# Transposes put at once instead of between matmuls, in the opening stage of a two-layer hybrid attention trunk

## The chip, the cores and the metric

One core of one Trainium2 chip runs the whole program. The metric is the device time of one execution in microseconds (us). Lower is better.

## The reference, cut to what matters

x and mem are 256 x 1024 in float32. Two layers, each with three branches on the same normalised input; the memory branch has keys and values that don't depend on x.

```python
for l in range(2):
    h = rmsnorm(x, norm_g[l])
    z = h @ w_in[l]                                  # 1024 x 7968, split into the inputs of the branches
    o_a = sparse_attention(...) * silu(...)
    o_b = forgetting_attention(...) * silu(...)
    mem_kv = rmsnorm(mem, mem_norm_g[l]) @ w_mem_kv[l]   # 1024 x 1024: keys, then values
    o_m = memory_attention(...) * silu(...)
    u = sum of g_i * (o_i @ w_branch_i[l])           # g_i = sigmoid of columns of z
    x = x + u @ w_out[l]
```

## The kernel before, in words

Every large product is done in three passes: an activation and a weight are each split into a high part (`aTh`, `whi`, a rounded copy) and a low part (`aTl`, `wlo`, what is left), and high x high, low x high and high x low are added in PSUM. A weight block of 256 rows is loaded by SyncE's queue into `wraw` (4 buffers), ScalarE writes `whi` (L168) and VectorE `wlo` (L169), 3 buffers each, two blocks ahead of use.

`gemm_steps` (L256) does one block: two row tiles t (128 rows of x or mem each) times two groups of 128 input channels times three passes, so 12 matmuls into one PSUM bank per t. `gemm` calls it four times for 1024 input channels. Tag `mm` has 3 banks, `S` 2, `T` 2, `O` 1. At the end of each step `tick` (L224) advances a clock and runs what `later(d, fn)` has put down as due.

Activations must lie transposed. `put_T` (L212) makes 4 transposes of 128 x 128 on TensorE into one bank of `T` (L220), and after the fourth calls the function that empties the bank: ScalarE writes the high part and VectorE the low part (L398 and L399, for two halves of the bank in turn). Each of these small pieces goes through `put` (L205) into the list `small`. `gemm_steps` hands the list out: after each of its matmuls it issues a share of what is in it (`hand_out`, L200), tied behind that matmul with `tc.issue_after`. `flush` (L196) issues the rest.

The tile framework orders each engine's instructions with a timeline simulation when the kernel is built (`schedule_with_timeline_sim=True`, L1248), so the order on an engine is the program's order as far as operands were ready in that simulation. In the trace it differs in places: matmuls of the values run before the last matmuls of the keys.

The opening stage, up to L643, in the program's order:

- 8 matmuls on zeros (L310), the gains `gk` transposed and copied (L333);
- `mem_norm` (L422): mem arrives in 4 column chunks of 256 channels. The first chunk is transposed at once and flushed. The other three (g = 1, 2, 3) hang on the list `within`: one is put down in the middle of each of the first three steps, between the 6 matmuls of t = 0 and the 6 of t = 1, so that its 4 transposes are handed out behind the matmuls of t = 1;
- `mem_stats` (L438): ScalarE squares the rows of mem (L443);
- `mem_kv` (L447): 4 steps for the keys, 4 for the values. From the keys' banks come squares (L366), a reciprocal root on GpSimd, the normalised keys (L457), and two `put_T` (after steps 5 and 6) whose banks are emptied into `mK` (L374, L376);
- `norm_x` (L629), due after step 1: squares of x (L633), x times its reciprocal root (L635), and four `put_T` after steps 4 to 7, whose banks are emptied into `hT`;
- `need(("h", l))`, and then the matmuls on `hT`: `K2` first, 416 columns wide.

So 9 calls of `put_T` lie between the first step and L643 of layer 0: 3 for mem, 4 for h and 2 for the keys, 36 transposes in all. All later use of `put` (attention units, and layer 1) goes on as it is.

Of the kernel before, what the change touches and what calls it, by code (L numbers as in the profile page):

```python
# [59 lines left out]
def hybrid_kernel(ctx: ExitStack, tc, I, cst_d, out_d):  # L60
# [131 lines left out]


    small = []

    def flush():  # L196
        while small:
            small.pop(0)()
# [6 lines left out]
    def put(*fns):  # L205

        def f():
            for fn in fns:
                fn()
        small.append(f)  # L210

    def put_T(blocks, then):  # L212

        q = []

        def one(i, b):
            if i == 0:
                q.append(pT())
            b = b()
            nc.tensor.transpose(q[0][0:b.shape[1], i * 128:(i + 1) * 128], b, ident)  # L220
        for i, b in enumerate(blocks):
            put(lambda i=i, b=b: one(i, b), *([lambda: then(q[0])] if i == len(blocks) - 1 else []))

    def tick():  # L224
        flush()
        clock[0] += 1
        unit_step()
        due = [c for c in conts if c[0] <= clock[0]]
        conts[:] = [c for c in conts if c[0] > clock[0]]
        for _, fn in due:  # L230
            fn()
# [16 lines left out]
    def need(k):  # L248
        for _ in range(60):
            if k in done_:  # L250
                flush()
                return
            tick()
        raise AssertionError(k)
# [220 lines left out]
    class Out:  # L475
# [4 lines left out]
        def add(self, cols, lhsT, rhs):  # L480
            def f():
                first = self.O is None
                if first:
                    self.O = pO()
                nc.tensor.matmul(self.O[0:lhsT.shape[1], cols], lhsT, rhs, start=first, stop=False,  # L485
                                 skip_group_check=True)
            put(f)

        def close(self):
            self.left -= 1  # L490
            if self.left == 0:
                add = small.pop()
                put(add, lambda: self.done(self.O))
# [80 lines left out]
    for l in range(2):  # L574
# [66 lines left out]
        mKT, mV = mem_kv(l, mT, rm)  # L641
        done_.discard("mem")
        need(("h", l))  # L643


        KH = S([128, 2, 2, T], "KH", dt=F32R)
# [605 lines left out]
```

## Time and profile before

| | |
|---|---|
| median of 3 runs | 646.13 us |
| the three runs | 644.62, 646.13, 646.20 us |
| the profiled execution | 645.26 us |
| its span, first to last instruction | 643.5 us |
| TensorE (PE) busy | 627.2 us, 97% |
| VectorE (DVE) busy | 484.5 us, 75% |
| ScalarE (ACT) busy | 391.8 us, 61% |
| GpSimd (POOL) busy | 173.8 us, 27% |
| mean granted clock of TensorE | 0.992 of full speed |

Times in the rows are us from the start of the span, unless ns is written. In a timeline row stand start, duration, engine, line, operation, what is written <- what is read, the count, and in brackets how long the engine had been idle and what ended that. A line of the program can be that of a helper: all transposes of `put_T` have L220 and all matmuls of `gemm_steps` L266. PE is the matmul side of TensorE, PEclk the granted clock as a share of full speed.

### The profile page before, as it was taken

To read this page: it belongs to the slowest core of one execution; us is meant where nothing else is said; L and a number is where in the kernel's file an instruction comes from. 1 tells how busy PE (TensorE), PEld (TensorE's weight loads), DVE (VectorE), ACT (ScalarE), POOL (GpSimd) and SP (SyncE) were. 2 spreads that over 40 slices of the span, in tenths; PEclk is the share of its full clock that TensorE was granted. 3 is DMA by queue.
4 is the path that set the end of the run, shared out by engine and by line. 5 is a ranking of instruction groups with operands and counts; after the bars stand their busy time and mean duration, and the time that the engine had idled before them with its cause. 6 is when DMAs were issued, how large, how long until landed. Compare 5 with 4: busy or idle time off the path is not lost.

```text
span 643.5 us, 10308 instructions
## 1 busy us (share of the span) xinstructions
PE 627.2 (97%) x3567; PEld 538.2 (84%) x3567; DVE 484.5 (75%) x849; ACT 391.8 (61%) x822; POOL 173.8 (27%) x232
## 2 busy tenths in 40 slices
PE   6889999999999999999999999999999999999997
PEld 4669898878898888888887989988889888888885
DVE  3567899867986886955586698996799688777563
ACT  5476578755667576654467566694467576765441
POOL 2531411441620420602112224122053041142030
PEclk7899999999999999999999999999999999999999
DMA  8746756765444644446754674576545355445542
GB/s 303 170 112 193 216 134 154 222 191 169 128 133 100 190 130 141 133 158 197 226 172 112 194 226 137 154 226 200 139 124 164 99 157 158 144 131 165 163 149 80
DMA packets 75412, 104.51 MB, mean 162 GB/s; under 512 B 16832, under 2 KB 31456, under 8 KB 75360
## 3 DMA queue, kind: packets, MB, share of 16 engines
q1 hardware_dynamic: 75296, 103.84, 55.6%
q8 instruction: 28, 0.46, 0.3%
q14 instruction: 24, 0.20, 0.1%
q10 hardware_dynamic: 64, 0.02, 0.0%
HBM read 102.78 MB, written 1.05 MB: 161 GB/s over the span
## 4 chain that ended last, share of the span: by engine, by line
PE 86%; DVE 6%; issue 2%; ACT 2%; DMA 2%; POOL 1%; SPq 0%; DVEq 0%; ACTq 0%
PE mm L266 60%; PE S L266 6%; PE T L220 5%; PE mm L820 5%; PE O L485 4%; DVE wlo L169 2%; PE S L1005 1%; DMA wraw<-in_w_mem_kv_dram 1%; PE S L1104 1%; PE S L1164 1%; DVE big L790 1%; PE S L911 1%; DVE sg L804 1%; ACT whi L168 1%; PE S L913 1%
## 5 line engine op out<-in xcount | busy, mean ns | idle before, releaser
L169 DVE TENSOR_TENSOR wlo<-wraw,whi 128x1024 fp32r<-128x1024 f32 (+3 forms) x185 | 231.2, 1254 | 88.6 <-ACT whi L168 87.3
L168 ACT ACTIVATE whi<-wraw 128x1024 fp32r<-128x1024 f32 (+3 forms) x185 | 192.3, 1041 | 111.6 <-PE mm L266 64.8
L266 PE MATMUL mm<-whi,aTh 128*128 128x512 f32 (+1 forms) x480 | 189.4, 401 | 7.3 <-ACT aTh L398 4.6
L266 PE MATMUL mm<-whi,aTl 128*128 128x512 f32 (+1 forms) x480 | 190.2, 396 | 1.3 <-DVE aTl L399 1.3
L266 PE MATMUL mm<-wlo,aTh 128*128 128x512 f32 (+1 forms) x480 | 184.4, 397 | 1.0 <-DVE wlo L169 1.0
L540 POOL TENSOR_TENSOR P<-P,d 128x512 f32<-128x512 f32 (+1 forms) x64 | 59.4, 944 | 209.1 <-DVE d L532 115.5
L266 PEld LDWEIGHTS mm<-whi,aTh 128*128 128x128 f32 x480 | 90.5, 190 | 25.4 <-ACT aTh L398 5.9
L266 PEld LDWEIGHTS mm<-wlo,aTh 128*128 128x128 f32 x480 | 91.1, 190 | 18.8 <-DVE wlo L169 1.9
L266 PEld LDWEIGHTS mm<-whi,aTl 128*128 128x128 f32 x480 | 91.1, 190 | 18.1 <-DVE aTl L399 1.7
L820 PE MATMUL mm<-aTh,wlo 128*128 128x256 f32 x192 | 54.8, 287 | 0.0
L820 PE MATMUL mm<-aTh,whi 128*128 128x256 f32 x192 | 54.7, 286 | 0.0
L820 PE MATMUL mm<-aTl,whi 128*128 128x256 f32 x192 | 54.6, 285 | 0.0
L529 ACT ACTIVATE P<-S,m 128x256 f32<-128x256 f32 (+1 forms) x112 | 46.8, 432 | 7.2 <-DVE m L526 6.5
L1078 POOL TENSOR_TENSOR big<-big,t 128x512 f32<-128x512 f32 x16 | 28.2, 1772 | 58.9 <-DVE t L1077 54.0
L374 ACT ACTIVATE PTh<-T 128x512 fp32r<-128x512 f32 (+1 forms) x48 | 26.8, 563 | 24.9 <-PE T L220 24.6
L266 PE MATMUL mm<-whi,oTh 128*128 128x512 f32 x96 | 38.5, 404 | 0.7 <-DVE t L1128 0.4
L266 PE MATMUL mm<-wlo,oTh 128*128 128x512 f32 x96 | 38.8, 407 | 0.0
L266 PE MATMUL mm<-whi,oTl 128*128 128x512 f32 x96 | 38.6, 403 | 0.0
L820 PEld LDWEIGHTS mm<-aTh,wlo 128*128 128x128 f32 x192 | 36.5, 191 | 0.4
L820 PEld LDWEIGHTS mm<-aTh,whi 128*128 128x128 f32 x192 | 36.6, 191 | 0.3
L820 PEld LDWEIGHTS mm<-aTl,whi 128*128 128x128 f32 x192 | 36.6, 191 | 0.2
L526 DVE TENSOR_REDUCE m<-S 128x2 f32<-128x512 f32 (+3 forms) x64 | 32.1, 515 | 2.7 <-PE S L1164 2.5
(236 smaller groups left out, 1030.5 us busy)
## 6 DMA issues: line engine op xcount, KB each, us to landing
wraw<-in_w_in_dram SPq DMA_DIRECT2D x112, 512.0 KB, 3.9
wraw<-in_w_out_dram SPq DMA_DIRECT2D x16, 512.0 KB, 4.1
wraw<-in_w_mem_kv_dram SPq DMA_DIRECT2D x15, 512.0 KB, 4.1
wraw<-in_w_branch_a_dram SPq DMA_DIRECT2D x16, 256.0 KB, 4.0
wraw<-in_w_branch_b_dram SPq DMA_DIRECT2D x8, 512.0 KB, 3.6
wraw<-in_w_branch_m_dram SPq DMA_DIRECT2D x8, 512.0 KB, 3.6
wraw<-in_w_in_dram SPq DMA_DIRECT2D x8, 408.0 KB, 3.2
wraw<-in_w_in_dram SPq DMA_DIRECT2D x8, 384.0 KB, 3.7
```

Source lines behind the costliest of these rows:

```text
L168: nc.scalar.activation(wh[:, j, :n], v[:, j, :n], AF.Copy)
L169: nc.vector.tensor_tensor(wl[:, j, :n], v[:, j, :n], wh[:, j, :n].bitcast(F32), op=ALU.subtract)
L220: nc.tensor.transpose(q[0][0:b.shape[1], i * 128:(i + 1) * 128], b, ident)
L266: mi = nc.tensor.matmul(o_, a[:, kg, ts], w_[:, k, :n], start=(kg == 0 and i == 0), stop=(last and k == 1 and i == 2))
L374: nc.scalar.activation(hi, src, AF.Copy, scale=scale)
L485: nc.tensor.matmul(self.O[0:lhsT.shape[1], cols], lhsT, rhs, start=first, stop=False, skip_group_check=True)
L526: nc.vector.tensor_reduce(m[:, n:n + c], heads(sp[:, o_:o_ + w * c], c), axis=AXX, op=ALU.max, negate=True)
L529: nc.scalar.activation(self.P[:, k], sp[:, k], AF.Exp, bias=m[:, n:n + 1], accum_out=d[:, n:n + 1])
L540: nc.gpsimd.tensor_tensor(P3, P3, b3(d[:, n:n + c], c, w), op=ALU.mult)
L790: nc.vector.tensor_tensor(QA[os_, g, :, ts], q[gs], QA[gs, g, :, ts].bitcast(F32), op=ALU.subtract)
L820: mi = nc.tensor.matmul(o_, w_, a[:, kg, :], start=(kg == 0 and j % 2 == 0 and i == 0), stop=(kg == 7 and i == 2), skip_group_check=True)
L1078: nc.gpsimd.tensor_tensor(uv, uv, tn, op=ALU.add)
```

## The change

A flag `lump` is true at first and becomes false for good after `need(("h", l))` of layer 0. While it is true, `put` issues its piece at once, in program order and tied to no matmul. After that it appends to `small` as before.

```diff
     small = []
+    lump = [True]
...
     def put(*fns):
 
         def f():
             for fn in fns:
                 fn()
-        small.append(f)
+        if lump[0]:
+            f()
+        else:
+            small.append(f)
...
         done_.discard("mem")
         need(("h", l))
+        lump[0] = False
```

## Rows read from the trace of the kernel before

**Rows 1.** The page: busy time of each engine over the span.
```profile
PE 627.2 (97%) x3567; PEld 538.2 (84%) x3567; DVE 484.5 (75%) x849; ACT 391.8 (61%) x822; POOL 173.8 (27%) x232
```
**Rows 2.** Windows: length; busy (count) PE, PEld, DVE, ACT, POOL; PEclk, DMA, GB/s.
```profile
0.00:45.50 45.50, 35.84 (x141) 26.37 (x142) 22.34 (x33) 26.11 (x53) 16.01 (x51) 0.89 0.69 197
...
8.70:15.10 6.40, 6.29 (x16) 4.25 (x16) 3.33 (x4) 4.76 (x9) 0.86 (x3) 0.52 1.04 395
...
22.00:26.70 4.70, 4.70 (x18) 3.46 (x17) 1.71 (x3) 1.43 (x3) 4.03 (x15) 0.67 0.88 126
26.70:33.30 6.60, 6.51 (x33) 5.13 (x31) 2.75 (x5) 3.22 (x9) 0.00 (x0) 1.00 0.79 207
33.30:36.50 3.20, 1.05 (x3) 0.59 (x4) 1.60 (x3) 3.20 (x14) 2.11 (x3) 1.00 0.00 0
```
**Rows 3.** Waits of PE from 3 to 45.5 us: total, times, longest.
```profile
PE mm L266 <- ACT aTh L398: 4.6, 3, 3.0
PE mm L266 <- ACT whi L168: 1.7, 1, 1.7
PE mm L266 <- DVE aTl L399: 1.3, 1, 1.3
PE mm L266 <- DVE wlo L169: 0.5, 1, 0.5
```
**Rows 4.** Timeline of PE in the opening stage.
```profile
8.77 1.22 PE L266 MATMUL mm<-whi,aTh 128*128 128x512 f32 x2 [2.96 <-ACT aTh L398]
...
12.99 0.41 PE L220 MATMUL T<-cst,big 128*128 128x128 f32 x1
...
16.36 0.73 PE L266 MATMUL mm<-whi,aTh 128*128 128x512 f32 x2 [1.31 <-ACT aTh L398]
...
20.86 0.50 PE L266 MATMUL mm<-whi,aTl 128*128 128x512 f32 x1 [1.31 <-DVE aTl L399]
...
32.62 0.60 PE L220 MATMUL T<-cst,t 128*128 128x128 f32 x4
...
45.50 0.43 PE L266 MATMUL mm<-whi,aTh 128*128 128x416 f32 x1
```
**Rows 5.** Timeline of ACT in the same stage.
```profile
12.74 1.04 ACT L443 ACTIVATE t<-big 128x1024 f32<-128x1024 f32 x1
...
15.86 0.45 ACT L398 ACTIVATE aTh<-T,gk 128x256 fp32r<-128x256 f32 x1
...
33.81 1.06 ACT L168 ACTIVATE whi<-wraw 128x1024 fp32r<-128x1024 f32 x1
```
**Rows 6.** Timeline of DVE in the same stage.
```profile
11.91 0.48 DVE L399 SCALAR_TENSOR_TENSOR aTl<-T,gk,aTh 128x256 fp32r<-128x256 f32 x1
...
18.37 0.76 DVE L635 TENSOR_SCALAR t<-x,rx 128x1024 f32<-128x1024 f32 x1 [0.71 <-DMA gcol<-in_fox_q_norm_dram]
19.04 1.38 DVE L169 TENSOR_TENSOR wlo<-wraw,whi 128x1024 fp32r<-128x1024 f32 x1
20.34 0.86 DVE L399 SCALAR_TENSOR_TENSOR aTl<-T,gk,aTh 128x256 fp32r<-128x256 f32 x2
...
36.44 0.68 DVE L457 TENSOR_TENSOR t<-mm,rmk 128x512 f32<-128x512 f32 x1
```
**Rows 7.** The chain that ended last, in order of time, merged pieces (start, length).
```profile
27.77 0.11 PE T L220
...
28.23 4.11 PE mm L266 x18
...
41.42 0.44 PE T L220 x4
```
**Rows 8.** SyncE's queue: the issue of mem's second chunk.
```profile
2.25 0.43 SPq L292 DMA_DIRECT2D big<-in_mem_dram  x1
```
**Rows 9.** DMA issues from 2.2 to 2.4 us: KB, us from issue to landing.
```profile
big<-in_mem_dram SPq DMA_DIRECT2D x1, 256.0 KB, 6.0
```
**Rows 10.** Windows of the matmuls of L266 alone: length; busy (count) PE, PEld; PEclk, DMA, GB/s.
```profile
8.70:32.60 23.90, 20.65 (x60) 12.67 (x60) 0.80 0.84 241
```

## The prediction, made before the change was run

> **What bounds the kernel now.** I read the page first, and from it one thing: TensorE is busy 627.2 of 643.5 us [rows 1], so PE sets the pace and only its own idle or slow time can be won. Next the windows. Of the 16.3 us in which PE isn't busy, 45.50 - 35.84 = 9.7 lie in the first 45.5 us, which is all that the change touches; the remaining 598 us have 6.6 us between them. The windows also show the second loss, the granted clock: 0.52 of full speed from 8.7 to 15.1 us (the lower of the two levels, 1.2 GHz, nearly throughout), and 0.67 from 22.0 to 26.7 [rows 2]. Third the waits of PE in the opening stage: three for the high part of the transposed activations (4.6 us), one for the low part (1.3), one each for a weight's two parts (1.7 and 0.5) [rows 3]. The timelines of PE, ACT and DVE then tell why the operand was late [rows 4 to 6].
>
> The reader should see this chain. Step 1 (keys, block 0) starts at 8.77. The transposes of mem's second chunk are handed out behind the matmuls of its second half and the last starts at 12.99, on a slow clock. By then ACT has gone into the squares of mem at 12.74, and the first half of that chunk is emptied only at 15.86; PE, done with step 1, stands still for 1.31 us until 16.36 [rows 4, 5]. The low part of the next half stands in DVE's queue behind x's normalisation (18.37) and a weight split (19.04) and comes at 20.34; PE stands still another 1.31 us until 20.86 [rows 4, 6]. Then the clock is low again for part of 22.0 to 26.7 [rows 2].
>
> **The change part by part.** It adds and removes no instruction and no DMA. It moves 36 transposes (9 calls of `put_T`) from "behind matmul n of the next half step" to "as early as the operand and the bank of tag `T` allow", ahead of those matmuls in the program's order. SyncE's queue gets nothing before or after anything else from it, and GpSimd neither. What moves with the transposes is the emptying on ACT and DVE.
>
> The transposes themselves: in the chain one between matmuls costs 0.11 us and four in a row cost 0.44, 0.11 each [rows 7]. So lump or not is worth 0; I take 0.
>
> *a, chunk 2 of mem.* Its data lie in memory at 2.25 + 6.0 = 8.25 us [rows 8, 9], inside the wait of 2.96 us that ends at 8.77 [rows 4]. At the low clock I double the 0.11 us: four transposes are 0.9 us that leave step 1. From 8.25 they would end near 9.1 and push the first matmul by up to 0.35. I take 0.5 us won, bounds 0 and 0.9.
>
> *b, the wait of 1.31 us before 16.36.* With the transposes done near 9, ACT can empty the bank before it enters the squares at 12.74, where it now comes behind them. Full removal is 1.3. If the first half still falls behind the squares, it is at best the first thing after two of them, 1 us sooner than 15.86. I take 1.0, bounds 0 and 1.3.
>
> *c, the waits of 0.35 (the third of the three for the high part, 4.6 - 2.96 - 1.31) and 1.31 us up to 20.86.* The second half of chunk 2 no longer waits; but chunk 3 goes into the bank that chunk 1 leaves after 11.91 + 0.48 = 12.4 us [rows 6], its emptying still meets squares on ACT and the split at 19.04 on DVE, and so a wait may come back one step later. I take half of 1.66: 0.8, bounds 0 and 1.66.
>
> *d, the low clock in 22.0 to 26.7.* At a mean of 0.67, (1 - 0.67) / 0.5 = 66% of 4.7 us ran at half pace, 3.1 us, half of which is lost: 1.5. It follows directly on the broken stretch before 20.86; from 26.7 to 36.5 the clock is full, although PE worked only 1.05 of the last 3.2 us [rows 2]. With the breaks mostly gone I take 1.0, bounds 0 and 1.5.
>
> *e, the end of the keys.* The chunk handed out last makes the fourth step of the keys late, and PE fills that time with matmuls of the values' first row tile: 60 matmuls of L266 stand between 8.7 and 32.6 [rows 10], the 48 of the keys and 12 of the values. That filling is then missing where PE stands still 1.7 and 0.5 us: the next `whi` is queued on ACT behind four squares of the keys and starts at 33.81 [rows 3, 5]. If the keys end sooner, those 12 matmuls come behind their end. At 4.11 / 18 = 0.228 us each [rows 7] they cover 2.7 us, more than the 2.2 of the two waits. I take 1.5, since ACT and DVE have the same work in less time; bounds 0 and 2.2.
>
> Six of the nine calls (h and the keys) need no more: their transposes already run mostly four in a row, as at 32.62 [rows 4], so for them the new order is near the old one. I cost this at nothing; what covers it is that PE has matmuls of the values whose operands are there.
>
> One rule of the Trainium skill speaks against the change. First the row: a lump of four at 32.62 followed by 1.7 us of standing still left the clock at 1.00 [rows 2 to 4]. The Trainium skill's page "TensorE: Matmul & The Clock Gate", section "Part 4: PE-mode transpose", says that a transpose does not count as work of the engine in the way a matmul does when its clock is granted. By that, transposes packed at the front of a step would hold the clock down longer; by the row they do no harm to a clock that is already up, and no row tells of one that is still low.
>
> Sum: 0.5 + 1.0 + 0.8 + 1.0 + 1.5 = 4.8 us. The profiled execution took 645.26, so it would take 640.5. The median of the runs shown is 0.9 above that execution, so against it 646.13 - 4.8 = 641.3. After 45.5 us the saving has nothing to disappear into: PE is idle there 6.6 of 598 us, weights are loaded when buffers come free, so they come sooner too. The order built by simulation may shift there; I allow 1 us either way. All bounds at their best give 0.9 + 1.3 + 1.66 + 1.5 + 2.2 = 7.6, or 638.5; all at zero 646.1.
>
> **The rivals.**
>
> *The wait changes its name.* ACT still does the squares of mem and x before it empties chunks 2 and 3, and DVE still does normalisation and weight split before the low parts; then steps 2 and 3 start where they do now. For it: the low part that ended the wait at 20.86 was late by DVE's queue, not by its transposes [rows 6]. Against it: the first one was done by PE only at 12.99 + 0.41, after ACT had entered the squares [rows 4, 5]. That leaves a and a part of b: 1.0 us, 645.1 by the median. This also holds the case that the built order stays nearly what it was. Chance 0.20.
>
> *Slower: a lump blocks PE.* Nothing ties a lump to a matmul any more, and PE takes its instructions in order. The place: the transposes of the keys, which need the normalised keys, there at 36.44 + 0.68 = 37.1 us, 4.5 after the keys' end near 32.6 [rows 4, 6]. If that lump is ordered ahead of the values' matmuls, PE stands 4.5 us instead of 2.2, so 2.3 more; and as the wait of 2.96 us before 8.77 was followed by 6.4 us at half pace [rows 2, 4], the clock would cost about 3.1 more. Against the 3.3 of a to d that is 646.13 - 3.3 + 2.3 + 3.1 = 648.2. It decides from the point where the added wait and its clock pass 3.3 us. Against it: before, the lumps from 32.62 on ran without a wait in front of them. Chance 0.08.
>
> *The clock stays low over step 2.* As a mechanism here: with four transposes moved in front of it, step 1 is matmuls on a low clock and the rise comes a step later. 12 matmuls at half pace cost 12 x 0.228 = 2.7 us, 646.13 - 4.8 + 2.7 = 644.0. The rule above would have it so. Against it: step 1 loses only the transposes and its matmuls then stand closer together. Chance 0.08, about evenly on both sides of 0.3%.
>
> **How the numbers follow.** Forecast 0.64, wait renamed 0.20, blocked PE 0.08, low clock 0.08. A measurement of this kernel can't tell under about 0.3% (1.9 us) from no change; the three runs spread 1.6. Faster: 0.64 and half of the low clock, and a little of the renamed wait where b comes out whole: 0.70. Same 0.22, slower 0.08. The likeliest case by itself reaches from 638.0 (all bounds, and half of the 1 us of order) to 644.0. The range takes in most of the renamed wait: 638.0 to 646.0.
>
> **What the profile after would show.** The first 416-wide matmul, at 45.50 now, near 40.7; the distance from it to the end unchanged within 1 us. Step a: transposes of the second chunk in front of the first matmul, or right behind it. Step b: an `aTh` of L398 on ACT ahead of L443, and no wait near 16. Step c: PE waiting less than 0.9 us between 16 and 22. Step d: a clock near 1.00 from about 16 on. Step e: L457 on DVE well before 36.44, and less than 1 us of waiting behind the keys' end. Wrong would be: the same waits at the same times with other releasers, a T matmul with a wait of its own in front of it, a low clock past 16, or a first 416-wide matmul near 41 with the end where it was.

## The result, and the profile after

Median 639.42 us (638.95 to 639.66, 4 runs) against 646.16 (644.62 to 646.26, 4 runs): ratio 0.9903 with a 95% interval of [0.9891, 0.9914], so 6.7 us or 1.0% faster. Measured a second time, the ratio was 0.9917 [0.9901, 0.9933] (639.64 us against a median of 645.17 over 22 executions of the kernel before, so 5.5 us). One execution of the kernel before (888.68 us) and one in experiment 6 (887.22 us) ran at a mean granted clock of 0.65 and are left out of all medians here. The forecast was 641.3, the range 638.0 to 646.0. The profiled execution took 639.60 us with a span of 637.9; before these were 645.26 and 643.5.

Windows of the changed kernel (columns as in [rows 2]):

```profile
8.80:11.00 2.20, 2.19 (x10) 1.80 (x10) 0.16 (x1) 0.93 (x1) 0.00 (x0) 0.72 1.08 393
11.00:13.20 2.20, 1.83 (x4) 0.50 (x2) 2.01 (x3) 1.89 (x5) 0.00 (x0) 0.50 1.03 404
13.20:19.50 6.30, 6.27 (x31) 4.87 (x31) 3.25 (x5) 6.30 (x14) 3.19 (x9) 1.00 0.86 311
19.50:26.70 7.20, 6.55 (x28) 4.77 (x29) 6.10 (x9) 3.88 (x7) 7.20 (x17) 1.00 0.62 93
...
39.30:637.90 598.60, 591.75 (x3431) 512.05 (x3429) 462.38 (x817) 366.11 (x770) 157.34 (x182) 1.00 0.55 160
```

The last line is the part behind the opening stage; in the kernel before it is this:

```profile
45.50:643.50 598.00, 591.36 (x3429) 511.80 (x3427) 462.15 (x817) 365.74 (x770) 157.81 (x182) 1.00 0.55 160
```

598.6 us now, 598.0 before: nothing was won or lost there beyond 0.6 us. The whole saving lies ahead of the first 416-wide matmul, which moved from 45.50 to 39.26. The clock is at its full level from 13.2 us on; the second low stretch (0.67 in 22.0 to 26.7, [rows 2]) is gone.

PE's waits from 3 to 45 us, and its timeline (L224 is now the transpose, L270 the matmul, L402 and L403 the emptying):

```profile
PE T L224 <- DMA big<-in_mem_dram: 2.2, 1, 2.2
PE mm L270 <- ACT whi L168: 0.9, 2, 0.6
PE mm L270 <- DVE wlo L169: 0.5, 1, 0.5
PE mm L270 <- ACT aTh L402: 0.3, 1, 0.3
```

```profile
8.81 0.63 PE L224 MATMUL T<-cst,big 128*128 128x128 f32 x4 [2.23 <-DMA big<-in_mem_dram]
9.19 0.71 PE L270 MATMUL mm<-whi,aTh 128*128 128x512 f32 x2
...
10.13 0.63 PE L270 MATMUL mm<-wlo,aTh 128*128 128x512 f32 x1
10.55 0.63 PE L270 MATMUL mm<-whi,aTl 128*128 128x512 f32 x1
...
14.25 0.40 PE L270 MATMUL mm<-whi,aTh 128*128 128x512 f32 x1
...
14.94 0.60 PE L224 MATMUL T<-cst,big 128*128 128x128 f32 x4
...
17.46 0.60 PE L224 MATMUL T<-cst,big 128*128 128x128 f32 x4
17.82 0.71 PE L270 MATMUL mm<-whi,aTh 128*128 128x512 f32 x2
...
39.26 0.35 PE L270 MATMUL mm<-whi,aTh 128*128 128x416 f32 x1
```

Chunk 2 is transposed in front of the first matmul, as soon as its data land. Behind 9 us the waits sum to 1.7 us; before, the same sum was 5.1 (4.6 + 1.7 + 1.3 + 0.5 - 2.96, [rows 3, 4]). The 13th large matmul starts at 14.25 (before 16.36), the 25th at 17.82 (before 22.05, by my count of both timelines).

ACT in the changed kernel. Each `aTh` empties half a chunk; in this order they are the second half of chunk 1 with the first of chunk 2 (merged), then chunk 2, 3, 3 with 4 (merged), 4:

```profile
11.03 0.82 ACT L402 ACTIVATE aTh<-T,gk 128x256 fp32r<-128x256 f32 x2
...
13.13 0.46 ACT L402 ACTIVATE aTh<-T,gk 128x256 fp32r<-128x256 f32 x1
13.48 1.05 ACT L447 ACTIVATE t<-big 128x1024 f32<-128x1024 f32 x1
...
16.60 0.46 ACT L402 ACTIVATE aTh<-T,gk 128x256 fp32r<-128x256 f32 x1
...
18.95 0.82 ACT L402 ACTIVATE aTh<-T,gk 128x256 fp32r<-128x256 f32 x2
...
21.95 0.48 ACT L402 ACTIVATE aTh<-T,gk 128x256 fp32r<-128x256 f32 x1 [1.23 <-DVE aTl L403]
...
26.54 0.37 ACT L370 ACTIVATE sq<-mm,rm 128x128 f32<-128x128 f32 x1 [0.69 <-PE mm L270]
```

And in the kernel before the second half of chunk 2, the two of chunk 3, the two of chunk 4 and the first squares of the keys:

```profile
18.20 0.46 ACT L398 ACTIVATE aTh<-T,gk 128x256 fp32r<-128x256 f32 x1
19.59 0.47 ACT L398 ACTIVATE aTh<-T,gk 128x256 fp32r<-128x256 f32 x1 [0.93 <-PE T L220]
21.23 0.47 ACT L398 ACTIVATE aTh<-T,gk 128x256 fp32r<-128x256 f32 x1 [1.17 <-DVE aTl L399]
...
25.96 0.47 ACT L398 ACTIVATE aTh<-T,gk 128x256 fp32r<-128x256 f32 x1 [3.04 <-PE T L220]
...
27.62 0.46 ACT L398 ACTIVATE aTh<-T,gk 128x256 fp32r<-128x256 f32 x1
...
32.42 0.37 ACT L366 ACTIVATE sq<-mm,rm 128x128 f32<-128x128 f32 x1 [2.15 <-PE mm L266]
```

This is where the gain builds up. The first half of chunk 2 is emptied about 4.5 us sooner (11.4 for 15.86). At chunk 3, which meets the squares of mem and x on ACT, 3.0 and 2.3 us of that are left (16.60 for 19.59, 18.95 for 21.23). At the last half of chunk 4 it is 5.7 us (21.95 for 27.62), because chunk 4's four transposes ran in a row at 17.46 us, where before they had been handed out from 22.90 to 25.66 behind matmuls that were late and on the low clock:

```profile
22.90 0.41 PE L220 MATMUL T<-cst,big 128*128 128x128 f32 x1
...
25.66 0.27 PE L220 MATMUL T<-cst,big 128*128 128x128 f32 x1
```

The keys' product of the first row tile, whose end releases the squares, ends 5.9 us sooner (26.54 for 32.42).

### The profile page after: what moved, and what is told of

Read it like the earlier page. It is cut to its first block, busy times and chain, and to the rows that moved or that the text cites. A ratio compares the mean times of both kernels' runs of the same rounds, so it can differ in the third digit from the quotient of the medians.

```text
span 637.9 us, 10306 instructions
## 1 busy us (share of the span) xinstructions
PE 625.4 (98%) x3567; PEld 536.3 (84%) x3567; DVE 484.2 (76%) x849; ACT 391.4 (61%) x822; POOL 174.6 (27%) x232
## 4 chain that ended last, share of the span: by engine, by line
PE 87%; DVE 6%; DMA 3%; ACT 2%; issue 2%; SPq 0%; DVEq 0%; ACTq 0%
PE mm L270 60%; PE S L270 6%; PE T L224 5%; PE mm L825 5%; PE O L489 4%; DMA wraw<-in_w_mem_kv_dram 2%; DVE wlo L169 2%; PE S L1010 1%; PE S L1109 1%; PE S L1169 1%; ACT whi L168 1%; DVE big L795 1%; PE S L916 1%; DVE sg L809 1%; PE S L918 1%
## 5 line engine op out<-in xcount | busy, mean ns | idle before, releaser
L270 PE MATMUL mm<-whi,aTh 128*128 128x512 f32 (+1 forms) x480 | 188.6, 399 | 2.2 <-ACT whi L168 1.2
L270 PE MATMUL mm<-whi,aTl 128*128 128x512 f32 (+1 forms) x480 | 188.7, 393 | 0.2
L270 PE MATMUL mm<-wlo,aTh 128*128 128x512 f32 (+1 forms) x480 | 182.9, 393 | 1.0 <-DVE wlo L169 1.0
L270 PEld LDWEIGHTS mm<-whi,aTh 128*128 128x128 f32 x480 | 90.0, 189 | 20.5 <-ACT whi L168 2.3
L270 PEld LDWEIGHTS mm<-wlo,aTh 128*128 128x128 f32 x480 | 90.4, 188 | 18.6 <-DVE wlo L169 1.9
L270 PEld LDWEIGHTS mm<-whi,aTl 128*128 128x128 f32 x480 | 90.4, 188 | 16.8 <-DVE aTl L403 1.3
L270 PE MATMUL mm<-whi,oTh 128*128 128x512 f32 x96 | 38.5, 404 | 0.6 <-ACT PTh L378 0.6
L270 PE MATMUL mm<-wlo,oTh 128*128 128x512 f32 x96 | 38.8, 407 | 0.0
L270 PE MATMUL mm<-whi,oTl 128*128 128x512 f32 x96 | 38.6, 403 | 0.0
```

The costliest lines, as they stand in the source:

```text
L270: mi = nc.tensor.matmul(o_, a[:, kg, ts], w_[:, k, :n], start=(kg == 0 and i == 0), stop=(last and k == 1 and i == 2))
```

## The experiments

Theory E: mem's chunks are emptied earlier, and that carries nearly all of it. Its rivals stand in the expectations.

**1 and 2: which calls.** One kernel makes lumps of mem's three chunks only, the other of h and the keys only.

```diff
     def f(g=g):
+        lump[0] = l == 0      # first kernel; the flag starts False. Second: False
         to_T_scaled(mT, lambda t: mrow[:, t, :], g, ...)
+        lump[0] = False       # second: l == 0
```

> Lumps only for the three calls of mem's chunks 2 to 4; the four of h and the two of the keys are handed out between matmuls as before. Theory E (the gain is the earlier emptying of mem's chunks: PE's waits at 16.4 and 20.9 and the two low-clock stretches): 639 to 640.5, nearly all of the 6.7 us. Theory H (the gain comes from the six calls of h and the keys, or from all nine in proportion): 643.9 to 646.

> The reverse: mem's chunks 2 to 4 are handed out between matmuls as before, h and the keys are put at once. Theory E: 645 to 646.5, no gain that can be told. Theory H: 639.5 to 642.

Measured 0.9939 [0.9923, 0.9955] (640.78) and 1.0008 [0.9997, 1.002] (645.42). mem carries most, though 640.78 is 0.28 us above what E allowed, and the ratio gives about two thirds of the gain where E says nearly all; h and the keys alone carry nothing that can be told.

**3 and 4: lump or freedom.** One keeps the lumps but ties each behind the next matmul; the other hands out one by one in the program's order, but without the tie.

```diff
-        if lump[0]: f()
-        else: small.append(f)
+        small.append(f)
...
     if small:
         with tc.issue_after(mi.ins):
-            hand_out(12 - t * 6 - k * 3 - i)
+            hand_out(1 if lump[0] else 12 - t * 6 - k * 3 - i)
```

```diff
-    if small:
+    if small and lump[0]:
+        hand_out(12 - t * 6 - k * 3 - i)
+    elif small:
         with tc.issue_after(mi.ins):
             hand_out(12 - t * 6 - k * 3 - i)
```

> All nine calls are lumps of four, but each still tied behind the next matmul that follows in the program. So the lump is kept and what is taken away is the freedom to go ahead of that matmul. Theory E says that only being early counts: the four of chunk 2 then end near 10.7 instead of 13.4 us, before the squares enter ACT at 12.7, so 640 to 642.5. Rival L (lumps as such are what helps): 639.4, as the changed kernel. Rival F (the freedom to run ahead, into the wait before the first matmul, is what helps): 644 to 646.

> The opposite of the one before: in the opening stage the pieces are again handed out one by one behind the matmuls in the program's order, but without the tie, so that the built order may pull them ahead. Theory E and rival F: 639.4 to 641, since chunk 2 is pulled into the wait before the first matmul. Rival L (lumps as such): 644 to 646, as before.

Measured 0.9929 [0.9915, 0.9944] (640.23) and 0.9953 [0.9938, 0.9968] (641.85, 0.85 us above what E allowed). Either one gives about half or more of the gain, and neither is necessary: rivals L and F in their strict form fall. Common to both is that the first half of chunk 2 is emptied early, at 12.64 in the first and 11.4 in the second, for 15.86 before.

**5 and 6: which chunk.** Lumps for chunk 2 alone (`lump[0] = l == 0 and g == 1` in `f`), or for chunks 3 and 4 alone (`g > 1`).

> Only chunk 2 of mem is put at once, chunks 3 and 4 and h and the keys as before. Theory E by its terms (the wait of 1.3 us at 16.4, the four transposes out of step 1, and a clock that rises about 3 us sooner, at half pace worth 1.5): 642.5 to 644. If the later waits (20.9, 22 to 25 at the low clock, 34.9) hang on chunk 2 as well: 640 to 641.5.

> Only chunks 3 and 4 of mem are put at once, chunk 2 as before. Theory E: the wait at 16.4 and the long low clock of step 1 stay, the break at 20.9 and the low clock from 22 to 25 go: 642 to 644. If chunk 2 carries all: 645 to 646.5.

Measured 0.9929 [0.9914, 0.9943] (640.48) and 0.9990 [0.9979, 1.0002] (643.79). Chunk 2 carries most of it; my sum of terms for it (642.5 to 644) was too small. For chunks 3 and 4 alone the time lies in the range of E, but the kernel before had 645.42 here, executions of both spread over 2 us and more, and the ratio tells no gain. With chunk 2 alone, chunks 3 and 4, though handed out as before, are early by themselves when step 1 isn't followed by a wait. ACT with chunk 2 alone, last half of chunk 4, its window over step 1, and PE in step 1 and at the first and last transpose of chunk 4:

```profile
23.01 0.47 ACT L402 ACTIVATE aTh<-T,gk 128x256 fp32r<-128x256 f32 x1 [1.29 <-DVE aTl L403]
```

```profile
8.80:13.10 4.30, 4.30 (x12) 3.21 (x13) 2.50 (x4) 3.33 (x6) 0.00 (x0) 1.00 1.04 395
```

```profile
10.97 0.63 PE L270 MATMUL mm<-wlo,aTh 128*128 128x512 f32 x1
11.39 0.63 PE L270 MATMUL mm<-whi,aTl 128*128 128x512 f32 x1
...
18.58 0.27 PE L224 MATMUL T<-cst,big 128*128 128x128 f32 x1
...
20.94 0.27 PE L224 MATMUL T<-cst,big 128*128 128x128 f32 x1
```

The clock of 1.00 in that window can't be taken as it stands: the matmuls of step 1 start 0.42 us apart (10.97, 11.39), just as in the changed kernel (10.13, 10.55), whose window says 0.72, and 0.23 us apart later (13.56 and 13.79 in the changed kernel). So step 1 ran at half pace here too, and so it did in the execution with chunks 3 and 4 (10.37, 10.79). These two experiments don't say what the clock of step 1 is worth.

**7 and 8: the clock alone.** `WARM = 12` in place of 8, in the kernel before and in the changed one.

> The kernel before with 12 instead of 8 matmuls on zeros at its start (4 more at 0.44 us, which end before the first operands are there). If the clock's rise only follows from how early TensorE is busy without a break, step 1 runs faster and 1 to 2 us go: 644 to 645.2. If step 1's clock depends on what comes after 8.8 us: 646, no change. It prices the clock alone, without the earlier emptying.

> The changed kernel with 12 instead of 8 matmuls on zeros. Step 1 runs at the low clock there from 8.8 to 13.1 us, so up to 2.1 us can be won: 637.3 to 638.5 if the clock is up by the first matmul, 639.4 if not, and 640 if the four matmuls delay the transposes of chunk 1.

Measured 0.9998 [0.9986, 1.0009] (645.06) and 0.9931 [0.9916, 0.9945] (640.71). No help for either: 645.06 lies in the range for a gain, but the kernel before had 645.42 beside it. What came of it was another test than I meant: on ACT the next weight block's `whi`, which waits 3.69 us for its data, now stands ahead of the emptying of chunk 1 (11.09, before 8.24), and the first large matmul starts at 11.60 instead of 8.77 in the kernel before. Even this 2.8 us late start costs nothing there that can be told: the wait behind step 1 takes most of it up, and the last half of chunk 4 is emptied 0.8 us later (28.43 for 27.62). In the changed kernel no such wait is left behind step 1. There, in experiment 8, the first large matmul starts at 11.41 instead of 9.19, and the six executions (640.04 to 641.05) all lie above the nine of the changed kernel (638.95 to 639.76).

```profile
10.12 1.06 ACT L168 ACTIVATE whi<-wraw 128x1024 fp32r<-128x1024 f32 x1 [3.69 <-DMA wraw<-in_w_mem_kv_dram]
```

```profile
11.60 1.22 PE L266 MATMUL mm<-whi,aTh 128*128 128x512 f32 x2 [4.50 <-ACT aTh L398]
```

```profile
11.41 1.22 PE L270 MATMUL mm<-whi,aTh 128*128 128x512 f32 x2 [2.29 <-ACT aTh L402]
```

**9: the changed kernel again**, beside 10 and 11.

> The changed kernel once more, beside the next two on the same chip and against more runs of the kernel before. Theory E: chunk 2 alone gave a ratio of 0.993, and chunks 3 and 4 with it should give a little more, so 639.4 (0.990). If the whole change is no better than chunk 2 alone: 640.5 (0.993).

Measured 0.9917 [0.9901, 0.9933] (639.64): its interval overlaps that of chunk 2 alone, so the ratios don't tell the two apart.

**10: another cure.** I had blamed mem's squares on ACT for the first wait. Here only they move, tied behind the emptying of chunk 2; the transposes are handed out as before.

```diff
-    rm = mem_stats(mrow0)
+    rm = []
+    def stats():
+        with tc.issue_after(last[0].ins):     # last: the latest aTh of L398
+            rm.extend(mem_stats(mrow0))
+    later(1, stats)
```

> The kernel before with its transposes handed out between matmuls as ever; only the two squares of mem on ACT (L443) are tied behind the emptying of chunk 2. Theory E says that what counts is when a chunk is emptied, not how its transposes are placed: the first half of chunk 2 is emptied near 13.5 instead of 15.9 us, the rest follows one step sooner, 640.5 to 643. Rival P (the placing of the transposes on TensorE itself, its waits and its clock): 645 to 646, no change.

Measured 1.0003 [0.9993, 1.0014] (644.92). My expectation fell, and no change is what rival P had forecast. ACT and PE of this kernel:

```profile
12.12 0.46 ACT L400 ACTIVATE aTh<-T,gk 128x256 fp32r<-128x256 f32 x1
13.90 0.48 ACT L400 ACTIVATE aTh<-T,gk 128x256 fp32r<-128x256 f32 x1 [1.32 <-DVE aTl L401]
14.28 1.05 ACT L445 ACTIVATE t<-big 128x1024 f32<-128x1024 f32 x1
...
18.35 0.45 ACT L400 ACTIVATE aTh<-T,gk 128x256 fp32r<-128x256 f32 x1
...
27.69 0.47 ACT L400 ACTIVATE aTh<-T,gk 128x256 fp32r<-128x256 f32 x1 [1.84 <-DVE aTl L401]
```

```profile
7.40 0.73 PE L266 MATMUL mm<-whi,aTh 128*128 128x512 f32 x2 [0.87 <-ACT aTh L400]
...
18.86 0.73 PE L266 MATMUL mm<-whi,aTh 128*128 128x512 f32 x2 [2.00 <-ACT aTh L400]
19.42 0.27 PE L220 MATMUL T<-cst,big 128*128 128x128 f32 x1
20.91 0.79 PE L266 MATMUL mm<-whi,aTl 128*128 128x512 f32 x1 [1.22 <-DVE aTl L401]
...
24.92 0.41 PE L220 MATMUL T<-cst,big 128*128 128x128 f32 x1
```

Chunk 2 is emptied as early as wished (12.12 and 13.90 for 15.86 and 18.20), but the squares now stand in front of chunk 3 (18.35), PE waits 2.00 and 1.22 us there, and chunk 4's transposes, each tied behind a matmul, take from 19.42 to 24.92, the later ones at the lower clock (0.41 for 0.27 us). The last half is emptied at 27.69, as before. In the kernel with chunk 2 as a lump the same four, also tied, took from 18.58 to 20.94. In this execution step 1 also started 1.4 us sooner than before and ran at the full pace (two matmuls in 0.73 us at 7.40, for 1.22 at 8.77), and that won nothing either. So an early chunk 2 is not enough. That the chain to chunk 4 has to hold is how I read the trace; it is not shown against rival P, since no run empties all of mem early with the transposes placed as before.

**11: an attempt to better the change.** The same tie of mem's squares, behind chunk 3, and `norm_x` due one step later (`later(2, norm_x)`), on the changed kernel.

> The changed kernel, with the squares of mem tied behind the emptying of chunk 3 and the normalisation of x due one step later. Theory E: in the changed kernel the first half of chunk 3 is emptied at 16.6 us, behind those squares; out of their way it can be near 15.5 and the last half sooner than 21.95, so 637.5 to 639.4. If by now the weights' arrival and splitting set the pace: 639.4. If the later normalisation makes h late: 640 to 642.

Measured 0.9998 [0.9988, 1.0008] (644.69): the whole gain is lost. The lump of h is now ordered ahead of its data, and blocks PE:

```profile
31.35 0.30 PE L224 MATMUL T<-cst,t 128*128 128x128 f32 x1 [1.92 <-DVE t L646]
32.79 0.55 PE L224 MATMUL T<-cst,t 128*128 128x128 f32 x3 [1.14 <-DVE t L646]
```

That is the rival "a lump blocks PE", which the change itself was spared, at another place: 3.1 us of waits in front of h's transposes instead of the keys', followed by a mean clock of 0.72 from 33.0 to 39.2 us, worth about (1 - 0.72) x 6.2 = 1.7 us. Together that is 4.8 of the 5.2 us by which the first 416-wide matmul is later (44.46 for 39.26). Chunk 4 was emptied 3.9 us late as well (25.88 for 21.95), but PE filled that time with matmuls of the values: its 60th large matmul starts only 0.7 us later (29.05 for 28.33).

**12: dose.** The changed kernel with the lump of chunk 4 made late again.

```diff
+            elif g == 3:
+                def tied():
+                    with tc.issue_after(last_mm[0].ins):   # the last matmul of step 3
+                        f()
+                later(3, tied)
             elif g:
                 within.append(f)
```

> The changed kernel with one lump made late again: the transposes of mem's chunk 4 are tied behind the last matmul of the keys' third step. So far the kernels whose last half chunk was emptied at 21.6 to 23.7 us took 639.6 to 642 and those at 25.9 to 28.4 took 644 to 646. If that moment is what sets the time, it should fall near 24.5 to 25.5 here and cost about as much as it is later than 22.0: 641.5 to 643. If it is the early chunk 2 that counts, whatever becomes of chunk 4 (the values' matmuls fill the gap): 639.4 to 640.3.

Measured 0.9944 [0.9928, 0.9961] (641.75), as the moment of the last emptying wants it, and outside what the other theory allowed (639.4 to 640.3). ACT: last half of chunk 4 (the first of the merged two).

```profile
25.12 0.87 ACT L404 ACTIVATE aTh<-T,gk 128x256 fp32r<-128x256 f32 x2 [0.97 <-DVE aTl L405]
```

All kernels together, each from its own profile: start of the last emptying of mem (ACT), start of the keys' squares (ACT; in 3, 4, 5, 8, 10 and 11 ACT came straight from other work or waited for something else, so the keys may have ended sooner), start of the first 416-wide matmul (PE), and the ratio to the kernel before:

```
kernel                        mem emptied  squares    first 416   ratio
before                        27.62        32.42      45.50       1
changed                       21.95        26.54      39.26       0.9903
1  lumps: mem only            21.86        26.49      39.20       0.9939
3  lumps, tied                22.67        27.38      40.09       0.9929
4  one by one, not tied       21.60        27.84      40.57       0.9953
5  lump: chunk 2 only         23.01        27.28      40.01       0.9929
8  changed, WARM = 12         23.65        28.20      40.92       0.9931
12 changed, chunk 4 late      25.12        28.11      42.18       0.9944
11 changed, squares behind    25.88        29.08      44.46       0.9998
6  lumps: chunks 3 and 4      26.02        31.01      43.67       0.9990
2  lumps: h and keys          26.23        31.03      44.10       1.0008
10 before, squares behind     27.69        31.17      43.91       1.0003
7  before, WARM = 12          28.43        33.25      45.95       0.9998
```

Every kernel whose keys' squares start by 28.2 us is faster, none of the others is. Among the faster ones no column gives the order of the ratios: 4 empties mem first of all and gains little more than half. Part of that is lost behind the opening: from the first 416-wide matmul to the end of the span kernels 1, 4, 6 and 11 took 599.6 to 600.0 us, the others 598.0 to 598.6. Each row is one execution, and the kernel before spreads over 3 us, so the rows of the kernels that are not faster can't be ranked.

## Why the prediction was right, point by point

*Where the bound is.* Right: PE sets the pace, the saving lies in the first 45 us and is carried to the end but for 0.6 us (598.0 and 598.6 behind it). The weights do stand in the way now: of the 1.7 us of waits left behind 9 us, 1.4 are for a weight's two parts.

*a, chunk 2 in the first wait, 0.5 us.* The move took place as described; the first large matmul came 0.42 us later (9.19 for 8.77), by the landing of chunk 2's data, a little more than the 0.35 allowed. A sign that I had called wrong, a T matmul with a wait of its own, is there with 2.23 us at 8.81, but it lies within the old wait of 2.96 us before step 1. Step 1 became 1.2 us shorter: 14.25 - 9.19 = 5.1, for 16.36 - 8.77 - 1.31 = 6.3 before, without the wait behind it. Less the 0.42, 0.8 were won, within the bounds. In the kernel before that time would have gone into the wait behind step 1, as the 2.8 us of experiment 7 did; it counts only because that wait is gone too.

*b and c, 1.0 and 0.8 us.* The waits went as predicted (1.31, 0.35 and 1.31 became 0.30 and 0.58). The 25th large matmul moved by 4.2 us, where a to c say 2.3: the three waits of 2.97 went whole, and I had taken 1.8 of them; a gave 0.8 for 0.5; the remaining 0.5 had no term. What had none either is the first low stretch of the clock: (1 - 0.52) x 6.4 = 3.1 us were lost by it before and (1 - 0.72) x 2.2 + (1 - 0.50) x 2.2 = 1.7 in the changed kernel, so 1.4 less, part of which is in a. The rest of the sum, d and e, was a little too large: from the 25th matmul to the first 416-wide one 2.0 us were won, where d and e say 2.5, so the two errors partly cancel. As an estimate for all of the opening, waits less by 3.4 us, and low clock less by 1.4 and, in 22.0 to 26.7, by 1.5, less the 0.42 of the late start, come to 5.9 of the 6.2 us that were won. Behind these terms stands a chain that I did not price as one: chunks 2 to 4 are each handed out behind matmuls that wait for the one before, as at chunk 4 from 22.90 to 25.66. And the cause given for b was incomplete: experiment 10 takes the squares out of the way of chunk 2 and wins nothing; by its trace the next chunk then meets them.

*d, the clock, 1.0 us.* The second low stretch vanished with the breaks ahead of it. By the windows it had cost 1.5 us; what it cost by itself was not measured, since no experiment took away the low clock alone. The rule on transposes and the clock (the Trainium skill's page "TensorE: Matmul & The Clock Gate", section "Part 4: PE-mode transpose") did no harm that any row shows: with lumps at 14.94 and 17.46 us the clock stayed at 1.00.

*e, the end of the keys, 1.5 us.* The two waits there fell from 2.2 to 0.32 + 0.52 = 0.84, so 1.4.

*Six calls at nothing.* Alone they give nothing (experiment 2). But with lumps for mem only the ratio is 0.9939, not 0.9903 or 0.9917, at the same opening (39.20 and 39.26): its profiled execution lost 1.2 us behind it (599.8 for 598.6), of which two waits, 0.25 and 0.33 us at 74 us, are in the timeline and not in that of the changed kernel. Whether these belong to the order that is built or to the lumps of h and the keys stays open.

*The rivals.* The renamed wait did not come. The blocked PE did not come in the change; experiment 11 shows that it was real: 3.1 us of it and about 1.7 us of low clock behind took the whole gain, where it was forecast to decide from 3.3 us of both. A clock that stays low over step 2 did not come.

In sum, 4.8 us were forecast; 5.7 were found between the two profiled executions, 6.7 between the first medians and 5.5 between the second.

## What to carry to other kernels

Work handed out piece by piece behind matmuls runs at the matmuls' pace; where those matmuls wait for just that work, each break delays the next piece, and here a low clock followed the breaks. A delay at the front can come back larger at the end of the chain (what the change won was 2.3 us at chunk 3 and 5.7 at chunk 4), or be taken up by a wait behind it (2.8 us in experiment 7). In a stage that is still filling, put such work as early as its data allow, and spread it only once the operands are ahead. Then price the chain as a whole, its waits and the low clock behind each of them, and not a part of each wait; and look what the freed engine meets next before moving one block out of the way.

## What the runs showed that I had not expected

The clock's row is no guide at the very start: it says 1.00 from 0 to 5.5 us, and yet the eight matmuls there took 0.47 us each (3.78 / 8), twice the 0.23 of those that follow each other at 13.56 and 13.79. Where step 1 of experiment 5 ran at that half pace the row says 1.00 as well. The starts of matmuls that follow each other without a wait are the safer sign.

```profile
0.00:5.50 5.50, 3.94 (x9) 2.66 (x9) 0.48 (x1) 1.28 (x1) 2.18 (x13) 1.00 0.56 173
```

```profile
1.50 3.78 PE L314 MATMUL S<-P 128*128 128x512 f32 x8 [1.50 <-DVE P L311]
...
13.56 0.39 PE L270 MATMUL mm<-wlo,aTh 128*128 128x512 f32 x1
13.79 0.40 PE L270 MATMUL mm<-whi,aTl 128*128 128x512 f32 x1
```

The kernel before spread over 643.3 to 646.4 us, the changed one stayed within 638.95 to 639.76 in nine. In experiment 12, which spread over 640.6 to 642.5, the profiled execution at 642.45 had a mean clock of 0.86 from 26.7 to 39.2 us, 3.5 us at half pace, worth 1.75. Whether the spread of the kernel before comes from such a stretch is not shown.
